# A decoder layer with pooling mixer and RWKV-7: the recurrent state added by an identity product, eight down products alone at the change of passes, the final norm of the first half issued later, two output tiles written ahead of a norm

## The chip, the cores and the metric

The kernel runs on one core of one Trainium2 chip. The metric is the device time of one execution in microseconds (us). The engines of the core work side by side, each through its own list of instructions in order: PE (TensorE, matrix products), DVE (VectorE), ACT (ScalarE), POOL (GpSimd) and SP (SyncE, which here only starts DMA transfers). PEld is the part of PE that loads weights; it works beside the products.

## What is computed

One layer for 1024 prompt tokens and 8 decode tokens, model width 1024, everything in fp32:

```
proj = rmsnorm(x) @ w_in                  # split into a pooling part and an RWKV part
pool = mean over trailing windows of 2/4/8/16 tokens, minus the token, times pool_w
rwkv: per head, token by token, with a 64x64 state S:
    sa = S @ a_t
    S  = S * w_t + sa b_t + v_t k_t       # w_t: decay
    y  = S @ r_t
x = x + concat(pool, rwkv) @ w_out
x = x + square(relu(rmsnorm(x) @ w_up)) @ w_down       # 1024 -> 4096 -> 1024
y = rmsnorm(x)
```

The outputs are y for prompt and decode tokens and the new states.

## The kernel before, in words

**Number format.** A product marked fp32r is cheap; an fp32 product costs more. The large products (projection `pj`, output `mx`, down `dn`) split each fp32 operand into a high and a low part and add three fp32r products (`gemm`, line 185). A weight tile arrives as `wr` (down, output, projection) or `a` (up), ACT writes its high part `wh` (line 94, the helper of all ACT work), DVE the low part `wl` (line 167 or 176). The small products of the recurrence are true fp32.

**Order.** The instructions are put in order by a list scheduler from the data they share; the order of the Python code is its priority, not the final order. Each engine then executes its list strictly in order.

**Stages.** (1) Projection and recurrence, up to about 466 us: the projection of one group of columns runs among the recurrence of the one before. The recurrence is cut into 8 units (4 pairs of heads, two halves of the tokens); `chain` runs one unit as 8 steps of 64 tokens, each step dependent on the one before, 64 steps in all. In a step, `SV` (128 x 128: two heads, block diagonal) is the state. `pq` = AR·SV goes to PSUM, ACT copies it to `Q`, `pa` = TT·Q goes to PSUM, ACT writes its diagonal blocks into `SV`, `pu` = BKT·SV goes to PSUM, and DVE writes the next state, `gam`·`pu` + `sg`. `sg` is `gam` times the old state, which ACT computes at the beginning of the step. `py` collects the output. All these PSUM tiles have the name `pcs` in the rows. Other PE work (projection, `bkt`, `vt` and others) is put between the products of a step by the scheduler.

(2) Up to about 568 us: the rest of the pooling mixer (`po`, with weights `pw`), the last unit, and the output projection of the first half of the tokens (`mx`).

(3) Output projection of the second half (`out_block`, 8 tiles m of two blocks each) with the second norm (`norm2`, sums `ss`, scale `rs2`) and the operands of the up product (`up_operands`) of the first half.

(4) The MLP in two passes over the halves: `up_pair(p)` is a seven-product scheme on blocks of `w_up` (products `b`, line 1014; combinations `a`, line 991; result `uh`, `ul`), and between its products it takes pieces of `down` (`dn`, added into `x` by DVE, line 1080) from a generator. Pairs 0 to 15 are the first half, 16 to 31 the second. At the change, `open_operands(1)` reloads the operands of the second half in 14 transfers on POOL's queue (line 932):

```
for t, d in zip(XO[half][i], XD[i]):
    GP.dma_start(t, d)
```

In group G == 7 four of the eight `down` tiles are drained ahead of `up_pair(16)`, and the other four are given to it. Behind that stands the final norm of two 256-column blocks of the first half (line 1086).

Of the kernel before, what the change touches and what calls it, by code (L numbers as in the profile page):

```python
# [7 lines left out]
F32 = mybir.dt.float32  # L8
F32R = mybir.dt.float32r
AF = mybir.ActivationFunctionType  # L10
ALU = mybir.AluOpType
# [4 lines left out]
P = 128  # L16
# [70 lines left out]
def _build(ctx, nc, tc, I, O, dbg):  # L87
    V, A, PE, SY, GP = nc.vector, nc.scalar, nc.tensor, nc.sync, nc.gpsimd
# [4 lines left out]
    def act(out, in_, func=AF.Copy, bias=0.0, scale=1.0, **k):  # L93
        A.activation(out, in_, func, bias=bias, scale=scale, **k)  # L94

    def open_pool(stack, name, bufs=1, **k):
        return stack.enter_context(tc.tile_pool(name=name, bufs=bufs, **k))

    R = (slice(0, 64), slice(64, 128))
# [13 lines left out]
    ident = cst[:, C_ID:C_ID + 128]  # L113
# [18 lines left out]
    def rstd(out, ps, ms, tmp):  # L132

        act(ms, ps, AF.Identity, bias=EPS6, scale=1.0 / D)
        act(tmp, ms, AF.Ln)
        act(out, tmp, AF.Exp, scale=-0.5)
        V.tensor_tensor(tmp, out, out, op=ALU.mult)
        V.scalar_tensor_tensor(tmp, tmp, -0.5, ms, ALU.mult, ALU.mult)
        V.scalar_tensor_tensor(out, tmp, 1.5, out, ALU.add, ALU.mult)
# [51 lines left out]
    rcp = open_pool(st_left, "rcp", reuse_waits="tile")  # L191
# [386 lines left out]
    def chain(U):  # L578
        hp = U.hp
        z1 = Zt[U.half][2]  # L580
        for i in range(2):
            nm = f"{hp}_{2 * U.half + i}"
            AR, RB, BKT, SV, TT = U.AR[i], U.RB[i], U.BKT[i], U.SV[i], U.TT
            if i == 0:
                for h in range(2):
                    if U.half == 0:
                        GP.memset(SV[R[h], 0, h, :], 0.0)
                    else:
                        act(SV[R[h], 0, h, :], Sf[hp][R[h], :])
            pyp = ps_y.tile([P, 512], F32, tag="y", name=f"py{nm}")  # L590
            py = pyp.rearrange("p (c h t) -> p c h t", h=2, t=64)
            for c in range(4):
                g = 4 * i + c
                gn = f"{U.nm}_{g}"
                sg = rcp.tile([P, 2, 64], F32, tag="sg", name=f"sg{gn}", bufs=2)
                act(sg, SV[:, c, :, :], scale=U.gam[:, g:g + 1])

                o = 256 * (hp % 2)
                pq, pa = (pcs[:, o + 128 * q:o + 128 * q + 128].rearrange("p (h t) -> p h t", t=64) for q in range(2))
                pu = pq  # L600
                PE.matmul(pq, AR[:, c, 0, :, :], SV[:, c, :, :], start=True, stop=True)  # L601
                PE.matmul(py[:, c, :, :], SV[:, c, :, :], AR[:, c, 1, :, :], start=True, stop=False)
                Q = rcp.tile([P, 2, 64], F32, tag="Q", name=f"Q{gn}", bufs=2)
                act(Q, pq)
                PE.matmul(pa, TT[:, g, :, :], Q, start=True, stop=True)  # L605
                for h in range(2):
                    act(SV[R[h], c, h, :], pa[R[h], h, :])
                PE.matmul(pu, BKT[:, c, :, :], SV[:, c, :, :], start=True, stop=True)  # L608
                PE.matmul(py[:, c, :, :], SV[:, c, :, :], RB[:, c, :, :], start=False, stop=True)
                for h in range(2):  # L610
                    if g == 7:
                        dst = Sf[hp][R[h], :]
                    elif c == 3:
                        dst = U.SV[1][R[h], 0, h, :]
                    else:
                        dst = SV[R[h], c + 1, h, :]
                    V.scalar_tensor_tensor(dst, pu[R[h], h, :], U.gam[R[h], g:g + 1], sg[R[h], h, :], ALU.mult, ALU.add)
            ys = rcp.tile([P, 256], F32, tag="ys", name=f"ys{nm}", bufs=2)
            for h in range(2):
                act(ys[R[h]].rearrange("p (c t) -> p c t", t=64), py[R[h], :, h, :])  # L620
            post(hp, nm, pyp, ys, 256, U.bv[:, 256 * i:256 * i + 256], z1[:, 256 * i:256 * i + 256], ys)
            QM.dma_start(mix_d[4 + hp][U.half][:, 256 * i:256 * i + 256], ys)
        if U.half:
            QM.dma_start(O["wkv_p"][hp], Sf[hp])
# [243 lines left out]
    def x1s(m, c, n):  # L868

        h = int(c >= 512)  # L870
        return x1[h][:, m, c - 512 * h:c - 512 * h + n]
# [39 lines left out]
    xtmp = lambda x, n: hq.tile([P, 260], F32, tag="xt", name=x, bufs=NXT)[:, :n]  # L911

    def norm2(c, n, tmp):

        ss = ps_m.tile([P, 512], F32, tag="m", name=f"ss2{c}")
        acc = tmp(f"acc2{c}")[:, :n]
        for m in range(KT):
            sq = tmp(f"sq2_{c}_{m}")[:, :n] if m else acc
            act(sq, x1s(m, c, n), AF.Square)
            if m:  # L920
                V.tensor_tensor(acc, acc, sq, op=ALU.add)
        PE.matmul(ss[:, :n], ON, acc, start=True, stop=True)
        rstd(rs2[:, c:c + n], ss[:, :n], tmp(f"ms2{c}")[:, :n], tmp(f"tt2{c}")[:, :n])
# [10 lines left out]
    def up_operands(half, k):  # L934

        c0, n = HALF[half]
        q = n // 2
        b = {}

        def normed(i, kk, o):  # L940
            b[i] = xtmp(f"b{i}_{k}_{half}", q)
            V.scalar_tensor_tensor(b[i], x1s(kk, o, q), col(V_G2, kk), rs2[:, o:o + q], ALU.mult, ALU.mult)

        def put(i, x):
            if half:
                h, l = (mp.tile([P, 260], F32R, tag=f"xs{y}", name=f"xs{i}{y}{k}", bufs=2) for y in "hl")
            else:
                h, l = (t[:, k, :q] for t in XO[half][i])
            act(h, x)
            V.tensor_tensor(l, x, f32(h), op=ALU.subtract)  # L950
            if half:
                for t, d in zip((h, l), XD[i]):
                    GP.dma_start(d[:, k, :], t)

        def less(i, x, y, out):
            V.tensor_tensor(b[out], b[x], b[y], op=ALU.subtract)
            put(i, b[out])

        normed("11", k, c0)
        put("11", b["11"])  # L960
        normed("21", k + 4, c0)
        put("21", b["21"])
        normed("12", k, c0 + q)
        less("t1", "12", "11", "11")
        normed("22", k + 4, c0 + q)
        put("22", b["22"])
        less("t2", "22", "11", "11")
        less("t3", "22", "12", "12")
        less("t4", "21", "11", "21")
# [80 lines left out]
    with tc.tile_pool(name="opb", bufs=1, reuse_waits="tile") as op:  # L1050
        ops = [mixed(op, k, 1, 3) for k in range(KT - 1)]
        load_x1(1)
        for c in (0, 256):
            norm2(c, 256, lambda x: xtmp(x, 260))
        open_operands(0)
        for m in range(KT):
            w = weights(I["w_out"][m, :, :(KT - 1) * P])
            for o in (0, 260):
                out_block(m, w, ops, 1, o, 260)
            if m % 2:  # L1060
                up_operands(0, m // 2)
        last = [mixed(op, KT - 1, 1, 3)]
        w7 = [w for m in (0, 4) for w in weights(I["w_out"][m:m + 4, :, (KT - 1) * P:].rearrange("m p c -> p m c"))]
        for m in range(KT):
            for o in (0, 260):
                out_block(m, w7[m:m + 1], last, 1, o, 260)
# [42 lines left out]
    for G in range(15):  # L1109
        first, rest = downs(G, range(4)), downs(G, range(4, 8))  # L1110
        if G == 1:
            for c, n in BLK[1:]:
                norm2(c, n, tmp)
        if 2 <= G < 6:
            up_operands(1, G - 2)
        if G == 7:
            open_operands(1)
            for _ in first:
                pass
        up_pair(2 * G + 2, rest if G == 7 else first)  # L1120
        up_pair(2 * G + 3, () if G == 7 else rest)
        if G == 7:
            for c in (0, 256):
                ss = ps_m.tile([P, 512], F32, tag="m", name=f"ss30{c}")[:, :256]
                acc = tmp(f"acc30{c}", "acc")[:, :256]
                for m in range(KT):
                    sq = tmp(f"sq3_{c}_{m}")[:, :256] if m else acc
                    act(sq, x1s(m, c, 256), AF.Square)
                    if m:
                        V.tensor_tensor(acc, acc, sq, op=ALU.add)  # L1130
                PE.matmul(ss, ON, acc, start=True, stop=True)
                for x in final_scale((c, 256), ss):
                    final(*x)
# [6 lines left out]
    for b in (1, 2):  # L1140
        c, n = BLK[b]
# [88 lines left out]
```

## Time and profile before

| | |
|---|---|
| median of 3 runs | 1336.54 us (1336.04 to 1337.41) |
| the profiled execution: its time, its span | 1335.81 us, 1334.0 us |
| mean granted clock of TensorE | 0.991 of full |
| PE busy | 1267.3 us, 95% of the span |
| PEld busy | 1146.4 us, 86% |
| DVE busy | 1050.9 us, 79% |
| ACT busy | 822.5 us, 62% |
| POOL busy | 125.4 us, 9% |
| DMA | 143.19 MB, mean 107 GB/s |

The span runs from the first to the last instruction of the profiled execution; some 1.8 us of its time lie around it. A row of the timeline gives start, duration, engine, line, operation, output<-inputs, shape, and in brackets how long the engine stood idle before it and what ended the wait. Shares of busy time are means over stages that are limited by different things.

### The profile page before, as it was taken

How to read it: one execution, taken by the hardware profiler on the slowest of the kernel's cores; microseconds unless marked ns; L12 is line 12 of the kernel's file. 1: busy time of each engine (PE TensorE's matmuls, PEld its weight loads, DVE VectorE, ACT ScalarE, POOL GpSimd, SP SyncE). 2: the span in 40 equal slices, each digit the busy share in tenths (PEclk: the TensorE clock that was granted, in tenths of full speed). 3: DMA queues.
4: the chain of work that ended last, by engine and by line, in shares of the span. 5: the costliest groups of instructions: out<-in, count | busy, mean ns of one | idle time of the engine just before them, and what ended most of it. 6: DMA issues, size and time to landing. Idle time of an engine off the chain costs nothing.

```text
span 1334.0 us, 27179 instructions
## 1 busy us (share of the span) xinstructions
PE 1267.3 (95%) x10230; PEld 1146.4 (86%) x10230; DVE 1050.9 (79%) x2331; ACT 822.5 (62%) x2015; POOL 125.4 (9%) x248
## 2 busy tenths in 40 slices
PE   5999999899999989989999999999899999999996
PEld 5987788798777867789989888998799999999996
DVE  8897687778877756589989997786698787878775
ACT  7668677776777657364757564555465645455552
POOL 4101001210011021110002320001000000000000
PEclk9999999999999989999999999999899999999999
DMA  6323123222222253442335663335634323332321
GB/s 209 102 54 83 43 50 90 95 93 53 66 56 48 63 164 135 142 149 80 119 115 150 181 167 96 113 97 186 217 99 147 103 89 105 94 106 93 104 71 64
DMA packets 119492, 143.19 MB, mean 107 GB/s; under 512 B 55769, under 2 KB 71257, under 8 KB 119353
## 3 DMA queue, kind: packets, MB, share of 16 engines
q1 hardware_dynamic: 97184, 92.22, 23.7%
q0 software_dynamic: 20320, 47.39, 11.4%
q10 hardware_dynamic: 1856, 1.85, 0.4%
q8 instruction: 80, 1.31, 0.4%
q14 instruction: 52, 0.42, 0.1%
HBM read 120.68 MB, written 20.97 MB: 106 GB/s over the span
## 4 chain that ended last, share of the span: by engine, by line
PE 68%; ACT 12%; DVE 11%; DMA 5%; issue 4%; POOL 1%; SPq 0%; DVEq 0%; ACTq 0%; POOLq 0%
PE dn L185 23%; PE b L1014 21%; PE pj L185 8%; PE mx L185 4%; ACT SV L94 2%; DMA a<-in_w_up 2%; PE pcs L608 1%; PE sc L431 1%; ACT wh L94 1%; ACT TT L94 1%; PE pcs L605 1%; DVE tm L525 1%; PE pcs L601 1%; DVE wl L167 1%; PE bkt L445 1%
## 5 line engine op out<-in xcount | busy, mean ns | idle before, releaser
L185 PE MATMUL dn<-uh,wh 128*128 128x260 f32 (+1 forms) x736 | 237.7, 324 | 6.1 <-DVE x L1080 4.3
L185 PE MATMUL dn<-ul,wh 128*128 128x260 f32 (+1 forms) x736 | 237.4, 323 | 1.2 <-DVE ul L1025 1.2
L185 PE MATMUL dn<-uh,wl 128*128 128x260 f32 (+1 forms) x736 | 237.2, 323 | 1.0 <-DVE wl L167 1.0
L94 ACT ACTIVATE wh<-a 128x512 fp32r<-128x512 f32 x192 | 120.8, 629 | 161.3 <-PE dn L185 85.0
L94 ACT ACTIVATE wh<-wr 128x512 fp32r<-128x512 f32 x230 | 142.9, 622 | 98.6 <-PE dn L185 26.0
L185 PE MATMUL pj<-xh,wh 128*128 128x258 f32 (+3 forms) x576 | 172.3, 299 | 13.7 <-ACT wh L94 13.7
L167 DVE TENSOR_TENSOR wl<-wr,wh 128x512 fp32r<-128x512 f32 x230 | 155.7, 681 | 35.4 <-ACT wh L94 27.5
L185 PE MATMUL pj<-xl,wh 128*128 128x258 f32 (+3 forms) x576 | 170.3, 296 | 0.0
L185 PE MATMUL pj<-xh,wl 128*128 128x258 f32 (+3 forms) x576 | 170.0, 295 | 0.1
L185 PEld LDWEIGHTS dn<-uh,wh 128*128 128x128 f32 x736 | 138.9, 189 | 17.3 <-ACT uh L94 3.2
L185 PEld LDWEIGHTS dn<-uh,wl 128*128 128x128 f32 x736 | 138.8, 189 | 12.3 <-DVE wl L167 1.2
L185 PEld LDWEIGHTS dn<-ul,wh 128*128 128x128 f32 x736 | 138.9, 189 | 10.8 <-DVE ul L1025 1.8
L176 DVE TENSOR_TENSOR wl<-a,wh 128x512 fp32r<-128x512 f32 x192 | 131.3, 684 | 6.2 <-ACT wh L94 3.6
L1080 DVE TENSOR_TENSOR x<-dn,x 128x260 f32<-128x260 f32 (+1 forms) x192 | 97.6, 511 | 41.5 <-PE dn L185 39.9
L185 PEld LDWEIGHTS pj<-xh,wh 128*128 128x128 f32 x576 | 109.9, 191 | 17.6 <-ACT wh L94 13.7
L185 PEld LDWEIGHTS pj<-xl,wh 128*128 128x128 f32 x576 | 110.0, 191 | 2.3 <-issue 1.9
L185 PEld LDWEIGHTS pj<-xh,wl 128*128 128x128 f32 x576 | 109.8, 191 | 1.8 <-issue 1.0
L94 ACT ACTIVATE c<-c 128x256 f32<-128x256 f32 (+1 forms) x128 | 53.1, 415 | 45.7 <-DVE c L1029 45.2
L991 DVE TENSOR_TENSOR a<-a,a 128x512 f32<-128x512 f32 x96 | 66.2, 689 | 19.0 <-DMA a<-in_w_up 17.5
L1025 DVE TENSOR_TENSOR ul<-u,uh 128x256 fp32r<-128x256 f32 (+1 forms) x128 | 53.6, 423 | 18.8 <-ACT uh L94 18.4
L185 PE MATMUL mx<-mh,wh 128*128 128x260 f32 (+1 forms) x192 | 64.9, 341 | 3.3 <-ACT mh L94 1.9
L185 PE MATMUL mx<-ml,wh 128*128 128x260 f32 (+1 forms) x192 | 63.6, 332 | 0.9 <-DVE ml L881 0.9
(421 smaller groups left out, 3388.6 us busy)
## 6 DMA issues: line engine op xcount, KB each, us to landing
a<-in_w_up SPq DMA_DIRECT2D x128, 256.0 KB, 2.6
wr<-in_w_down SPq DMA_DIRECT2D x128, 256.0 KB, 2.6
wr<-in_w_in POOLq DMA_DIRECT2D x72, 256.0 KB, 3.1
wr<-in_w_out POOLq DMA_DIRECT2D x26, 256.0 KB, 3.2
xr<-in_xT SPq DMA_DIRECT2D x16, 256.0 KB, 3.6
mr<-mix SPq DMA_DIRECT2D x8, 260.0 KB, 4.3
x<-in_xT SPq DMA_DIRECT2D x4, 520.0 KB, 5.0
blk<-AA SPq DMA_DIRECT2D x16, 128.0 KB, 2.7
```

Of the source, the lines that this page charges most:

```text
L94: A.activation(out, in_, func, bias=bias, scale=scale, **k)
L167: V.tensor_tensor(l[:, :w], raw[:, :w], f32(h[:, :w]), op=ALU.subtract)
L176: V.tensor_tensor(l, raw, f32(h), op=ALU.subtract)
L185: PE.matmul(ps, lhs, rhs, start=i == 0, stop=i == n - 1)
L431: PE.matmul(psc[:, c, :], BK[:, c, 2 * h:2 * h + 2, :], AR[:, c, :, h, :], start=True, stop=True)
L445: PE.transpose(pt[:, c, :], BK[:, c, 2 * h:2 * h + 2, :].rearrange("p a t -> p (a t)"), ident)
L525: V.tensor_tensor(pr[:, q], l[:, q].unsqueeze(2).to_broadcast([64, m, m, m]), r[:, q].rearrange("p k j -> p j k").unsqueeze(1).to_broadcas ...
L601: PE.matmul(pq, AR[:, c, 0, :, :], SV[:, c, :, :], start=True, stop=True)
L991: V.tensor_tensor(a[out], a[x], a[y], op=op)
L1014: PE.matmul(ps, lhs[:, c], rhs, start=k == i == 0, stop=k == 3 and i == 2)
L1025: V.tensor_tensor(ul, u, f32(uh), op=ALU.subtract)
L1080: V.tensor_tensor(d, ps[:, :n], d, op=ALU.add)
```

## The change

Four edits. In `chain` the tile `sg` is gone; the old state is added by a product of the identity matrix with `SV`, as first product of the group in `pu`, and DVE only multiplies by `gam`. In the output projection of the second half, `norm2` of the first half is written behind tiles 0 and 1, and the four `up_operands` behind tiles 3, 5, 6 and 7. In group 7 all eight `down` tiles are drained ahead of `up_pair(16)`. The final norm of the first half stands at group 9.

```
-                sg = rcp.tile([P, 2, 64], F32, tag="sg", name=f"sg{gn}", bufs=2)
-                act(sg, SV[:, c, :, :], scale=U.gam[:, g:g + 1])
...
                 PE.matmul(pa, TT[:, g, :, :], Q, start=True, stop=True)
+                PE.matmul(pu, ident, SV[:, c, :, :], start=True, stop=False)
                 for h in range(2):
                     act(SV[R[h], c, h, :], pa[R[h], h, :])
-                PE.matmul(pu, BKT[:, c, :, :], SV[:, c, :, :], start=True, stop=True)
+                PE.matmul(pu, BKT[:, c, :, :], SV[:, c, :, :], start=False, stop=True)
...
-                    V.scalar_tensor_tensor(dst, pu[R[h], h, :], U.gam[R[h], g:g + 1], sg[R[h], h, :], ALU.mult, ALU.add)
+                    V.tensor_scalar(dst, pu[R[h], h, :], U.gam[R[h], g:g + 1], None, ALU.mult)
...
-        for c in (0, 256):
-            norm2(c, 256, lambda x: xtmp(x, 260))
         open_operands(0)
         for m in range(KT):
...
-            if m % 2:
-                up_operands(0, m // 2)
+            if m == 1:
+                for c in (0, 256):
+                    norm2(c, 256, lambda x: xtmp(x, 260))
+            if m > 2 and m != 4:
+                up_operands(0, (0, 1, 2, 3)[(3, 5, 6, 7).index(m)])
...
             for _ in first:
                 pass
-        up_pair(2 * G + 2, rest if G == 7 else first)
-        up_pair(2 * G + 3, () if G == 7 else rest)
-        if G == 7:
+            for _ in rest:
+                pass
+        up_pair(2 * G + 2, first)
+        up_pair(2 * G + 3, rest)
+        if G == 9:
```

The scheduler decides where this lands. On PE, the third step of one unit in the recurrence, before (L605 is `pa`, L608 `pu`; `pj` and `vt` are other work):

```order
L601 MATMUL pcs<-SV_0_1709,AR_137 128x128
L602 MATMUL py_0_3513<-AR_137,SV_0_1709 128x128
L449 MATMUL vt_1_2392<-cst,v_0_2058 128x128
L185 MATMUL pj_1_2628<-xh_205,wl 128x256
L185 MATMUL pj_1_2654<-xh_205,wh 128x256
L185 MATMUL pj_1_2654<-xl_206,wh 128x256
L605 MATMUL pcs<-Q_0_2_3544,TT_157 128x128
L185 MATMUL pj_1_2654<-xh_205,wl 128x256
L185 MATMUL pj_1_2654<-xh_205,wh 128x256
L185 MATMUL pj_1_2654<-xl_206,wh 128x256
L185 MATMUL pj_1_2654<-xh_205,wl 128x256
L608 MATMUL pcs<-SV_0_1709,BKT_0_1708 128x128
```

and the same step of the change, where the lines are L599, L603 and L607 and the identity product is L604 (`cst` holds the identity):

```order
L599 MATMUL pcs<-SV_0_1701,AR_137 128x128
L600 MATMUL py_0_3497<-AR_137,SV_0_1701 128x128
L185 MATMUL pj_1_2638<-xh_205,wh 128x256
L185 MATMUL pj_1_2638<-xl_206,wh 128x256
L603 MATMUL pcs<-Q_0_2_3524,TT_157 128x128
L604 MATMUL pcs<-SV_0_1701,cst 128x128
L185 MATMUL pj_1_2638<-xh_205,wl 128x256
L185 MATMUL pj_0_2695<-xh_171,wh 128x256
L185 MATMUL pj_0_2695<-xl_172,wh 128x256
L185 MATMUL pj_0_2695<-xh_171,wl 128x256
L607 MATMUL pcs<-SV_0_1701,BKT_0_1700 128x128
L608 MATMUL py_0_3497<-RB_141,SV_0_1701 128x128
```

The identity product stands directly behind `pa`, ahead of the other work.

On ACT, the end of the squares (`sq`) and the scale (`ms`, `tt`, `rs`) of the second norm among the operands `mh` of the output projection of the second half, before:

```order
L94 ACTIVATE sq_0_7_7147<-x_6510 128x256
L94 ACTIVATE ms_7151<-ss_7126,sm 128x256
L94 ACTIVATE mh_1_7081<-mr_1_7080 128x520
L94 ACTIVATE tt_7152<-ms_7151 128x256
L94 ACTIVATE mh_1_7087<-mr_1_7086 128x520
L94 ACTIVATE rs_7059<-tt_7152 128x256
L94 ACTIVATE mh_1_7093<-mr_1_7092 128x520
```

and of the change:

```order
L94 ACTIVATE sq_0_7_7213<-x_6446 128x256
L94 ACTIVATE ms_7217<-ss_7192,sm 128x256
L94 ACTIVATE mh_1_7017<-mr_1_7016 128x520
L94 ACTIVATE tt_7218<-ms_7217 128x256
L94 ACTIVATE mh_1_7023<-mr_1_7022 128x520
L94 ACTIVATE rs_6995<-tt_7218 128x256
L94 ACTIVATE mh_1_7029<-mr_1_7028 128x520
```

Only the numbers of the tiles differ.

On DVE at the change of passes, from the sum of the last `down` tile of group 6 (`dn_7`) to that of the first of group 7 (`dn_0`), before (`c` belongs to the last pair of the first half, `a_16` is a combination of `w_up` for the first pair of the second half):

```order
L1080 TENSOR_TENSOR x_6510<-dn_7_0_11968,x_6510 128x512
L167 TENSOR_TENSOR wl<-wr,wh 128x512
L1029 TENSOR_TENSOR c_15_11999<-u_15_11914,b_15_11982 128x256
L176 TENSOR_TENSOR wl<-a_16_12142,wh 128x512
L991 TENSOR_TENSOR a_16_12142<-a_16_12144,a_16_12142 128x512
L1025 TENSOR_TENSOR ul_11781<-u_15_12001,uh_11780 128x256
L1029 TENSOR_TENSOR c_15_12023<-u_15_11953,b_15_12006 128x256
L176 TENSOR_TENSOR wl<-a_16_12148,wh 128x512
L991 TENSOR_TENSOR a_16_12148<-a_16_12148,a_16_12142 128x512
L1025 TENSOR_TENSOR ul_11779<-u_15_12025,uh_11778 128x256
L1080 TENSOR_TENSOR x_6510<-dn_0_0_12064,x_6510 128x512
```

and of the change:

```order
L1080 TENSOR_TENSOR x_6446<-dn_7_0_11904,x_6446 128x512
L167 TENSOR_TENSOR wl<-wr,wh 128x512
L1028 TENSOR_TENSOR c_15_11935<-u_15_11850,b_15_11918 128x256
L167 TENSOR_TENSOR wl<-wr,wh 128x512
L1028 TENSOR_TENSOR c_15_11959<-u_15_11889,b_15_11942 128x256
L1024 TENSOR_TENSOR ul_11717<-u_15_11937,uh_11716 128x256
L167 TENSOR_TENSOR wl<-wr,wh 128x512
L1024 TENSOR_TENSOR ul_11715<-u_15_11961,uh_11714 128x256
L1080 TENSOR_TENSOR x_6446<-dn_0_0_12000,x_6446 128x512
```

The four rows on `a_16` are gone from between the `c` and `ul` rows of the last pair, and two more low parts of `down` weights stand there.

## Rows read from the trace of the kernel before

**Rows 1.** The page: the share of the span in which PE was busy, and the shares of the engines in the chain that ended last.
```profile
PE 1267.3 (95%) x10230; PEld 1146.4 (86%) x10230; DVE 1050.9 (79%) x2331; ACT 822.5 (62%) x2015; POOL 125.4 (9%) x248
PE 68%; ACT 12%; DVE 11%; DMA 5%; issue 4%; POOL 1%; SPq 0%; DVEq 0%; ACTq 0%; POOLq 0%
```

**Rows 2.** Busy time by stage. Columns: stretch, its length, then busy time (number of instructions) of PE, PEld, DVE, ACT, POOL, the granted clock of PE, the DMA share, GB/s.
```profile
66.00:466.00 400.00, 379.44 (x3805) 325.39 (x3804) 313.40 (x777) 292.80 (x823) 45.98 (x95) 1.00 0.25 66
466.00:568.00 102.00, 93.10 (x651) 71.87 (x650) 58.36 (x122) 56.73 (x176) 17.28 (x32) 0.95 0.48 150
568.00:627.00 59.00, 54.60 (x426) 52.01 (x427) 54.85 (x135) 30.59 (x70) 4.74 (x8) 1.00 0.39 123
921.00:961.00 40.00, 35.51 (x184) 29.66 (x183) 22.55 (x44) 16.78 (x35) 7.42 (x14) 0.91 0.82 272
```

**Rows 3.** The timeline of PE in one step of the recurrence (start, duration).
```profile
349.01 0.49 PE L608 MATMUL pcs<-SV,BKT 128*128 128x128 f32 x2
349.34 0.39 PE L609 MATMUL py<-RB,SV 128*128 128x128 f32 x2
349.56 0.60 PE L445 MATMUL bkt<-cst,BK 128*128 128x128 f32 x4
...
350.37 0.46 PE L601 MATMUL pcs<-SV,AR 128*128 128x128 f32 x2
350.67 0.39 PE L602 MATMUL py<-AR,SV 128*128 128x128 f32 x2
350.89 0.38 PE L445 MATMUL bkt<-cst,BK 128*128 128x128 f32 x2
351.20 0.49 PE L605 MATMUL pcs<-Q,TT 128*128 128x128 f32 x2
```

**Rows 4.** The timeline of ACT in the same step.
```profile
350.48 0.39 ACT L94 ACTIVATE sg<-SV,gam 128x128 f32<-128x128 f32 x1
350.87 0.28 ACT L94 ACTIVATE Q<-pcs 128x128 f32<-128x128 f32 x1
```

**Rows 5.** The timeline of PE and ACT in another step, in which `sg` had ended early.
```profile
203.77 0.39 PE L601 MATMUL pcs<-SV,AR 128*128 128x128 f32 x2
204.19 0.28 ACT L94 ACTIVATE Q<-pcs 128x128 f32<-128x128 f32 x1 [0.26 <-PE pcs L601]
204.52 0.49 PE L605 MATMUL pcs<-Q,TT 128*128 128x128 f32 x2
```

**Rows 6.** Groups of instructions over the span: count | busy us, mean ns of one | idle us of the engine before them, and what ended most of it.
```profile
L608 PEld LDWEIGHTS pcs<-SV,BKT 128*128 128x128 f32 x128 | 19.9, 190 | 19.3 <-ACT SV L94 18.3
L605 PEld LDWEIGHTS pcs<-Q,TT 128*128 128x128 f32 x128 | 19.7, 188 | 12.0 <-ACT Q L94 7.2 <-ACT TT L94 2.3 <-issue 0.2
L601 PEld LDWEIGHTS pcs<-SV,AR 128*128 128x128 f32 x128 | 20.3, 188 | 11.0 <-DVE SV L617 6.7 <-issue 1.0 <-DVE Sf L617 0.4
L94 ACT ACTIVATE sg<-SV,gam 128x128 f32<-128x128 f32 x64 | 25.0, 396 | 20.4 <-DVE SV L617 20.1
L617 DVE SCALAR_TENSOR_TENSOR SV<-pcs,gam,sg 64x64 f32<-64x64 f32 x112 | 31.7, 283 | 27.3 <-PE pcs L608 26.0
L525 DVE TENSOR_TENSOR tm<-Xs,tw 64x64 f32<-64x64 f32 x16 | 3.6, 256 | 0.2
```

**Rows 7.** Around the start of the output projection of the second half: the window 565 to 570 us (columns as in rows 2), rows of PE's timeline, and two issues on SP's queue.
```profile
565.00:570.00 5.00, 1.84 (x9) 1.14 (x9) 2.75 (x5) 3.19 (x8) 0.54 (x1) 1.00 0.68 200
566.90 0.67 PE L922 MATMUL ss<-acc,cst 128*128 128x256 f32 x2 [1.78 <-DVE acc L921]
568.72 0.51 PE L185 MATMUL mx<-mh,wh 128*128 128x260 f32 x2 [1.15 <-ACT mh L94]
564.91 0.38 SPq L866 DMA_DIRECT2D x<-in_xT  x1
569.43 0.32 SPq L879 DMA_DIRECT2D mr<-mix  x1
```

**Rows 8.** The handover from projection to output: a window and a row of PE's timeline.
```profile
475.00:480.00 5.00, 0.58 (x65) 0.48 (x55) 0.69 (x1) 3.25 (x9) 0.33 (x1) 0.83 0.98 365
479.96 2.10 PE L783 MATMUL po<-d,pw 128*128 128x256 f32 x4 [4.42 <-DMA pw<-in_pool_w]
```

**Rows 9.** The change of passes: the first of the 14 reloads on POOL, rows of DVE's and PE's timelines, and two pieces of the chain of waits (start, length, what).
```profile
921.61 0.53 POOL L932 DMA_DIRECT2D x11l<-xd11l  x1 [127.69 <-PE b L1014]
939.41 0.69 DVE L991 TENSOR_TENSOR a<-a,a 128x512 f32<-128x512 f32 x1 [5.03 <-DMA a<-in_w_up]
948.28 0.69 DVE L176 TENSOR_TENSOR wl<-a,wh 128x512 fp32r<-128x512 f32 x1
941.78 0.47 PE L185 MATMUL dn<-uh,wh 128*128 128x512 f32 x1 [0.67 <-DVE x L1080]
945.45 0.48 PE L185 MATMUL dn<-uh,wh 128*128 128x512 f32 x1 [2.04 <-DVE x L1080]
949.76 1.22 PE L185 MATMUL dn<-uh,wh 128*128 128x512 f32 x2 [1.78 <-ACT uh L94]
949.76 9.96 PE dn L185 x36
978.08 13.01 PE b L1014 x108
```

**Rows 10.** The final norm of the first half: eight instructions of DVE, and the wait of PE behind them.
```profile
996.72 3.25 DVE L1086 SCALAR_TENSOR_TENSOR x<-x,vec,rs 128x256 f32<-128x256 f32 x8
1000.70 0.39 PE L185 MATMUL dn<-uh,wh 128*128 128x260 f32 x1 [1.59 <-DVE x L1080]
```

## The prediction

> **What bounds the kernel now.** I read the page first, then the busy time by stage, then the timelines where the change works. PE is busy 95% of the span and makes up 68% of the chain that ended last, ACT and DVE some 12% each [rows 1]: work taken from ACT or DVE is worth time only where PE waits for it, and work added to PE costs time wherever PE does not wait. The stages say where that is [rows 2]. In the recurrence, 66 to 466 us, PE works 379.4 of 400 us at full clock, so 20.6 us are all that could be won there, though the chain of 64 steps runs through it. From 466 to 568 us it loses 8.9 us, in the output projection of the second half 4.4 us, at the change of passes 4.5 us of 40 at a granted clock of 0.91. These four places are the ones that the edits touch.
>
> **The identity product.** 64 products of 128x128 by 128x128 in fp32 are added to PE. The price is in the timeline of one step, from start to start of neighbouring fp32 products of that size: 350.67 to 350.89 and 349.34 to 349.56, 0.22 us, and 0.33 us where the first of two has just ended a wait (349.01 to 349.34) [rows 3]. The new one follows `pa` directly, so it is a running stream: 0.22 us, 64 x 0.22 = 14.1 us. The bounds are 64 x 0.33 = 21.1 us, and nothing, if it only filled a wait. Can it? PE does wait for ACT's write of `SV` ahead of the third product of a step, 18.3 us in all [rows 6]. But the identity product reads the whole of `SV`, the old state, and ACT overwrites blocks of the same tile. ACT therefore has to wait until the product has read it. The order shows the product immediately behind `pa` and the other work behind it, in about the former number. So ACT starts 0.22 us later, `SV` comes 0.22 us later, and the wait keeps its length behind the new work. I take the full 14.1 us. The identity stands in `cst` already, so nothing is loaded for it.
>
> **What ACT gives back.** `sg` takes 25.0 us of ACT, 64 x 0.396 [rows 6], and starts when DVE has written the state, as `pq` does; `Q` waits behind it. In the step at 350 us `sg` ends at 350.87 and `Q` starts then, 0.50 us after its product started (350.37) [rows 3, 4]. In the step at 204 us, with ACT free, `Q` starts 0.42 us after its product (203.77 to 204.19) [rows 5]. So 0.08 us are saved in a step, 64 x 0.08 = 5.1 us. Nothing (where other ACT work holds `Q` up, or PE has work to cover it) and 7.2 us (all that PE's weight loads wait for `Q` [rows 6]) are the bounds.
>
> **What DVE gives back.** The new `tensor_scalar` reads PSUM and a scalar per partition, and is not in the trace of before in that form. The old instruction takes 283 ns with one tile from PSUM and one from SBUF; an addition of two 64x64 tiles takes 256 ns [rows 6]. A second operand is no large part of either; I take 27 ns less, the distance of the two rows. Two such instructions end a step, 2 x 27 ns x 64 = 3.5 us; they matter where PE waits for DVE's state, 6.7 us, so not in every step, and I take 1.5 us. Bounds: nothing, and the 6.7 us. The Trainium skill, page "VectorE: DVE Perf Modes", section "Why PSUM operands drop a tier", says that an fp32 operand in PSUM keeps DVE at its slowest mode whatever else is read; by it the term is zero and the sum 1.5 us higher. No run here shows yet which of the two holds.
>
> **The norm and the out tiles.** The loss is real: in 565 to 570 us PE works 1.84 us of 5, first waiting for the sum of squares, then for `mh` [rows 7]. If the two tiles ran ahead of the norm, they would fill it. The order of the change, however, has on ACT the same sequence as before, the squares, `ms`, then the first `mh`, word for word but for tile numbers; the scheduler puts the norm in front again, since it is ready and the tiles are not. They need `x` and `mr`, whose transfers SP issues only at 564.91 and 569.43 us [rows 7]. So this edit is worth nothing, and its cover is not taken away either. The bounds are the loss in that window, 3.2 us, and with the whole loss of the following stage [rows 2] 3.2 + 4.4 = 7.6 us.
>
> **The handover.** Before the output projection PE stands still from about 475.5 to 480 us, at the end waiting 4.42 us for the pooling weights `pw`, while the DMA engines are full (0.98) [rows 8]. The scheduler shuffles work there (part of the last unit's small products, and two `mr` loads earlier on SP). What is issued to the full DMA engines does not become less; I take 0, with that wait as the bound on either side, 4.4 us.
>
> **The change of passes.** The 14 reloads begin at 921.61 us on POOL [rows 9] and fill the DMA engines (share 0.82 over 40 us [rows 2]). The combinations of `w_up` come late: DVE stands still 5.03 us until 939.41 us for one. DVE then has its queue to work off, and PE waits 0.67, 2.04 and 1.78 us for DVE's `x` and for the last `uh` [rows 9]: 4.5 us, the whole loss of the stage. The clock of 0.91 costs another 0.09 x 40 = 3.6 us, together 8.1 us. What do eight down products ahead change? The order on DVE has the same late `a` rows ahead of `x<-dn_7`; behind it, four rows on `a_16` of 0.69 us each [rows 9] give way to two `wl<-wr`, so the last `ul` comes 2 x 0.69 = 1.4 us sooner. I take 1.4 us; the bounds are all 8.1 us, and a loss of 1.4 us if the two `down` weights now needed sooner are late in the full DMA engines. Behind that nothing is to be won: the three down products that PE works off from 949.76 us cover the reloads already, and `b` then follows without a wait. The four downs that leave `up_pair(16)` are the same instructions in another place, and the pairs alone run as tightly as up products did before where they stood alone, 108 products in 13.01 us [rows 9].
>
> **The final norm.** Eight DVE instructions in one piece of 3.25 us hold up the sums of `dn`, and PE waits 1.59 us behind them [rows 10]. At group 9 the same eight stand among the same kind of work. 0, with 1.6 us either way.
>
> **The sum.** 14.1 - 5.1 - 1.5 - 1.4 = +6.1 us, from the profiled 1335.81 us to 1341.9. The median of the runs is 0.73 us above the profiled execution, so **1342.6 us** on that scale.
>
> **The rivals.**
> (a) Nothing is given back. PE has other work in most steps, and a `Q` that comes 0.08 us sooner finds PE at a product of 0.3 us. That wait for `Q` is 7.2 us of 400 speaks for it. +14.1: 1350.6 us.
> (b) DVE gains nothing from the lost operand, by the form of the instruction: 14.1 - 5.1 - 1.4 = +7.6: 1344.1 us. This is what the page on DVE would make of it.
> (c) The other side: the identity product lies in a wait after all. If ACT's write does not stand behind it, or the scheduler's filling shrinks by as much in the steps where PE idles (18.3 us in all ahead of `pu`), its effective price is zero and the time falls to 1336.54 - 8.0 = 1328.5 us. It decides from a price below 0.125 us a product (8.0 / 64), and makes the kernel measurably faster below 0.08. Against it stands that the product reads what ACT then writes.
> (d) The change of passes loses its whole stall because DVE has only weights of `down` to split: 14.1 - 5.1 - 1.5 - 8.1 = -0.6: 1335.9 us. Against it: DVE is late because of `a` rows that stand ahead in both.
> (e) The two tiles do run ahead of the norm on the chip: 6.1 - 3.2 to 6.1 - 7.6, 1339.4 to 1335.0 us. Against it stands the order.
>
> **How the numbers follow.** A difference under 0.2% (2.7 us) can't be told from none here, so the borders are 1333.9 and 1339.2 us. Chances: the forecast 0.33 (own range 1338 to 1346), (a) 0.18, (b) 0.12, (c) 0.15, (d) 0.12, (e) 0.10. Faster: 0.13 of (c), 0.03 of (d), 0.01 of (e), together 0.17. The same: 0.06 of the forecast, 0.02 of (c), 0.09 of (d), 0.06 of (e), together 0.23. Slower: the rest, 0.60. The range is 1333 to 1351 us: it leaves out (c) for the most part and the upper end of the price of the product, and holds the others.
>
> **What would show it.** In the new profile PE's busy time in the recurrence grows by 14 us and its stretch by about 7.5 us; PE's idle time ahead of `pu` on ACT's `SV` stays near 18 us; that ahead of `pa` falls by some 5 us of the 7.2 for `Q`; the DVE instruction reads near 256 ns. The window at 565 us looks as before, and the waits at 941 to 950 us are there, shorter by about 1.4 us. The prediction is wrong if the stretch of the recurrence does not grow, if PE's wait for `SV` shrinks by as much as the new products take, or if the change of passes moves by more than 3 us.

## The result: slower by 1.2%, more than twice the forecast loss

The changed kernel takes 1352.11 us in the median of 4 runs (1349.59 to 1355.3), the kernel before 1336.88 us (1336.04 to 1337.41). The ratio is 1.0118, 95% interval [1.0103, 1.0133], or some 15.8 us. The forecast was +6.1 us. The profiled execution of the change is its fastest, 1349.59 us (span 1347.8, clock 0.992); the other runs of it had granted clocks of 0.983 to 0.987.

First the page of the change, the same parts as [rows 1]:

```profile
PE 1281.3 (95%) x10358; PEld 1160.8 (86%) x10358; DVE 1050.2 (78%) x2331; ACT 804.8 (60%) x1951; POOL 125.2 (9%) x248
PE 69%; ACT 9%; DVE 7%; issue 7%; DMA 4%; POOL 2%; POOLq 0%; DVEq 0%; SPq 0%; ACTq 0%
```

PE worked 14.0 us longer, with 128 instructions more (64 fp32 products of two each), and the span grew by 13.8 us. ACT worked 17.7 us less and DVE 0.7 us less.

By stage, cut at the last product of the projection and at the same later places. Before (columns as in [rows 2]):

```profile
56.00:471.70 415.70, 395.10 (x3926) 340.11 (x3925) 326.48 (x806) 299.99 (x838) 48.16 (x100) 1.00 0.26 66
471.70:568.00 96.30, 87.40 (x605) 66.17 (x603) 55.14 (x116) 54.66 (x172) 15.65 (x29) 0.95 0.46 151
```

and of the change (the third row answers to the third of [rows 2]):

```profile
56.40:483.10 426.70, 407.38 (x4038) 352.46 (x4037) 326.96 (x806) 285.00 (x781) 47.57 (x100) 1.00 0.25 64
483.10:580.90 97.80, 88.69 (x621) 67.40 (x620) 54.87 (x116) 52.87 (x165) 16.11 (x30) 0.97 0.49 152
580.90:638.20 57.30, 55.21 (x426) 53.13 (x427) 54.64 (x135) 30.26 (x70) 4.72 (x8) 0.97 0.39 126
```

The recurrence grew by 11.0 us: PE's busy time by 12.28 us for 56 added products (112 instructions), 0.219 us each, while PE's idle time there went from 20.6 to 19.3 us. The next stretch grew by 1.5 us, the output projection of the second half became 1.7 us shorter. Between their last row and the end lie 707.0 us before and 709.6 us after; with 0.4 us at the start these make the 13.8 us.

What PE waited for in a step, and what DVE's instruction takes now (L607, L603, L599 are `pu`, `pa`, `pq`; columns as in [rows 6]):

```profile
L607 PEld LDWEIGHTS pcs<-SV,BKT 128*128 128x128 f32 x128 | 19.6, 190 | 19.0 <-ACT SV L94 17.8 <-issue 0.5 <-ACT tailS L94 0.2
L603 PEld LDWEIGHTS pcs<-Q,TT 128*128 128x128 f32 x128 | 20.0, 190 | 12.5 <-ACT Q L94 7.7 <-ACT TT L94 1.5 <-issue 0.5
L599 PEld LDWEIGHTS pcs<-SV,AR 128*128 128x128 f32 x128 | 19.9, 189 | 7.7 <-DVE SV L616 4.0 <-issue 1.0 <-ACT SV L94 0.4
L616 DVE TENSOR_SCALAR SV<-pcs,gam 64x64 f32<-64x64 f32 x112 | 31.7, 283 | 33.2 <-PE pcs L607 31.7
```

The wait for `SV` is as long as before, 17.8 instead of 18.3 us. The wait for `Q` did not fall, 7.7 instead of 7.2 us. DVE takes 283 ns, exactly as before. The wait for DVE's state fell from 6.7 to 4.0 us all the same.

At the change of passes, PE and ACT of the change (answering to PE's rows in [rows 9]):

```profile
953.52 0.47 PE L185 MATMUL dn<-uh,wh 128*128 128x512 f32 x1 [0.52 <-DVE x L1080]
957.18 0.47 PE L185 MATMUL dn<-uh,wh 128*128 128x512 f32 x1 [2.04 <-DVE x L1080]
963.22 0.79 PE L185 MATMUL dn<-uh,wh 128*128 128x512 f32 x1 [4.87 <-ACT uh L94]
```

```profile
961.34 0.63 ACT L94 ACTIVATE wh<-wr 128x512 fp32r<-128x512 f32 x1 [2.03 <-DMA wr<-in_w_down]
961.88 0.40 ACT L94 ACTIVATE c<-c 128x256 f32<-128x256 f32 x1
962.31 0.42 ACT L94 ACTIVATE u<-c 128x256 f32<-128x256 f32 x1
962.75 0.42 ACT L94 ACTIVATE uh<-u 128x256 fp32r<-128x256 f32 x1
```

The wait for the last `uh` was 1.78 us and is 4.87 us. The last `uh` stands on ACT behind the high part of a `down` weight whose transfer landed late.

### The profile page after: what moved, and what is told of

Same layout as the page of the kernel before. It is cut to its first block, busy times and chain, and to the rows that moved or that the text cites. A ratio compares the mean times of both kernels' runs of the same rounds, so it can differ in the third digit from the quotient of the medians.

```text
span 1347.8 us, 27412 instructions
## 1 busy us (share of the span) xinstructions
PE 1281.3 (95%) x10358; PEld 1160.8 (86%) x10358; DVE 1050.2 (78%) x2331; ACT 804.8 (60%) x1951; POOL 125.2 (9%) x248
## 3 DMA queue, kind: packets, MB, share of 16 engines
q0 software_dynamic: 20320, 47.39, 11.4%
## 4 chain that ended last, share of the span: by engine, by line
PE 69%; ACT 9%; DVE 7%; issue 7%; DMA 4%; POOL 2%; POOLq 0%; DVEq 0%; SPq 0%; ACTq 0%
PE dn L185 21%; PE b L1013 18%; PE pj L185 9%; PE mx L185 6%; PE pcs L607 2%; PE sc L431 2%; ACT SV L94 2%; PE pcs L603 1%; ACT TT L94 1%; PE pcs L599 1%; DVE tm L525 1%; DMA a<-in_w_up 1%; ACT wh L94 1%; DVE x L1086 1%; PE bkt L445 1%
## 5 line engine op out<-in xcount | busy, mean ns | idle before, releaser
L185 PE MATMUL pj<-xh,wh 128*128 128x258 f32 (+3 forms) x576 | 173.0, 300 | 14.6 <-ACT wh L94 14.1
L185 PEld LDWEIGHTS pj<-xh,wh 128*128 128x128 f32 x576 | 110.0, 191 | 18.6 <-ACT wh L94 14.1
L990 DVE TENSOR_TENSOR a<-a,a 128x512 f32<-128x512 f32 x96 | 66.1, 689 | 19.4 <-DMA a<-in_w_up 17.9
```

The source lines that it names most:

```text
L185: PE.matmul(ps, lhs, rhs, start=i == 0, stop=i == n - 1)
L990: V.tensor_tensor(a[out], a[x], a[y], op=op)
```

## The experiments

All times are against the kernel before on the same chip; us are worked out from the ratio.

**Which edit.** The first edit alone, and the other three without it:

```
e1: sg and its add removed, identity product added      e2: norm order, eight downs, final norm
```

> Only the first edit: the identity product, without `sg` and with the shorter DVE instruction; the other three edits are left out. Theory A (the product costs its whole PE time, 64 x 0.22 = 14.1 us, and ACT and DVE give nothing back): +12 to +15 us against before. Theory B (ACT and DVE give back the 6.6 us that were predicted, and the other edits lose as much): +6 to +8.5 us.

Measured: 1.0123 [1.0106, 1.0141], +16.4 us, above the upper end of theory A.

> The other three edits without the first. Theory A (the identity product is nearly the whole loss): -1.5 to +2.5 us against before, with about +2.4 us at the change of passes, -1.6 us in the output projection of the second half and -0.5 us from the final norm, as between the two traces. Theory B (half of the loss is in these edits): +6 to +9 us.

Measured: 1.0017 [1.0006, 1.0028], +2.3 us. The identity product is nearly the whole loss; theory B falls. Each of the three others alone:

> Only the second edit, the norm and the up operands written later. If the order on the chip stays in front and only the later up operands help: -1 to -2 us, all of it before the first down product. If it does nothing, as predicted: within 0.5 us.

Measured: 0.9998 [0.9985, 1.0012]. Nothing that can be told. The 1.7 us won in the change's output projection don't appear as a gain of this edit.

> Only the third edit, eight down products alone. Theory: `uh` waits on ACT behind the high parts of `down` weights whose transfers land late among the 14 reloads; PE's wait for `uh` grows from 1.8 to about 4.9 us and the kernel loses 2 to 3 us. As predicted it would gain 1.4 us.

Measured: 1.003 [1.0017, 1.0042], +4.0 us. In its trace PE waits 2.86 us for `uh`, one us more than before, where 3 were expected; the profiled execution was 1336.92 us, the fastest of 12, so the trace shows the loss smaller than the runs do. The traces of e1 and e8, with four downs as before, have 2.70 us, so this wait alone does not show the loss:

```profile
943.71 0.47 PE L185 MATMUL dn<-uh,wh 128*128 128x512 f32 x1 [2.04 <-DVE x L1080]
947.74 0.79 PE L185 MATMUL dn<-uh,wh 128*128 128x512 f32 x1 [2.86 <-ACT uh L94]
```

> Only the fourth edit, the final norm at group 9. If the stall behind the norm only moves: within 1 us of before, the waits of about 2.6 us at 1000 and 1021 us gone and about as much in the pairs 22 and 23.

Measured: 1.0001 [0.9989, 1.0014]. The stall moves. In the trace of the change it is at pairs 22 and 23:

```profile
1100.68 0.39 PE L185 MATMUL dn<-uh,wh 128*128 128x260 f32 x1 [0.80 <-DVE x L1080]
1119.81 0.39 PE L1013 MATMUL b<-xt2h,wh 128*128 128x260 f32 x1 [0.60 <-ACT wh L94]
1120.98 0.39 PE L185 MATMUL dn<-uh,wl 128*128 128x260 f32 x1 [0.67 <-DVE wl L167]
```

**The price of the product, apart from what is given back.**

```
e3: -  act(sg, SV[:, c, :, :], scale=...)        # and tensor_scalar in place of the add of sg
e4: +  PE.matmul(pu, ident, SV[:, c, :, :], start=True, stop=True)      # behind pa
e5: +  PE.matmul(pa, ident, SV[:, c, :, :], start=True, stop=True)      # behind py, end of the step
```

> `sg` is gone and DVE only multiplies, but no identity product is added: the old state is left out of the sum, so the output is not the reference's. It measures what ACT and DVE give back, alone. Theory A: -1.5 to +0.5 us against before, the wait of PE for `Q` stays near 7 us. Theory B: -5 to -8 us, that wait falls to about 2 us.

Measured: 0.999 [0.9978, 1.0001], -1.3 us, not to be told from none. PE's wait for `Q` is 6.3 us: theory A. Its recurrence, and that wait (L602 is `pa` here):

```profile
56.50:470.50 414.00, 394.60 (x3927) 340.15 (x3926) 328.14 (x806) 282.61 (x781) 47.97 (x100) 1.00 0.25 66
L602 PEld LDWEIGHTS pcs<-Q,TT 128*128 128x128 f32 x128 | 19.9, 188 | 11.7 <-ACT Q L94 6.3 <-ACT TT L94 2.3 <-issue 0.2
```

> `sg` and the DVE instruction stay as before; the identity product is added at the place that it has in the change, into `pu`, and the next product overwrites it. It measures the price of the product alone. Theory A: +12.5 to +15 us, with 0.22 us more from `pa` to `pu` in a step. Rival C (it lies in a wait): under +5 us.

Measured: 1.0148 [1.0134, 1.0161], +19.8 us: more than both theories said.

> As the one before, but the added product stands behind the last product of the step, reads the new `SV` and writes the place of `pa` that nobody reads any more: the same PE work, outside of the chain of a step. If PE's time alone sets the price (PE is nearly always busy): +12.5 to +15 us, as inside the chain. If the price comes from the longer step (ACT's write waits 0.22 us more): +3 to +8 us, since the product then fills PE's waits.

Measured: 1.0089 [1.0075, 1.0104], +11.9 us, a little under the first alternative. But the product did not land outside of the chain. DVE waits for it (L610) before it writes the next state (L618):

```profile
L618 DVE SCALAR_TENSOR_TENSOR SV<-pcs,gam,sg 64x64 f32<-64x64 f32 x112 | 31.7, 283 | 23.2 <-PE pcs L610 19.4 <-PE vt L449 2.1
```

In all 64 steps that write starts at least 0.31 us behind the second instruction of the added product; it starts 0.83 us (median) behind the second instruction of `pu`, where it was 0.31 us before. So e5 also lengthens the step, at its end, and a product outside of the chain was not tested. By the runs the product is 8 us dearer behind `pa` than at the end of the step. The recurrence does not show that difference. Windows up to the last product of the projection, and on to the second half's output projection, of e4 and then of e5:

```profile
56.00:488.20 432.20, 408.99 (x4039) 355.31 (x4038) 326.49 (x805) 301.29 (x838) 47.98 (x100) 0.99 0.24 63
488.20:589.00 100.80, 88.33 (x621) 66.64 (x619) 55.06 (x116) 54.55 (x174) 15.93 (x30) 0.95 0.48 147
```

```profile
56.00:488.20 432.20, 410.02 (x4037) 355.99 (x4036) 327.34 (x806) 299.79 (x837) 47.80 (x99) 0.99 0.25 65
488.20:583.40 95.20, 89.35 (x621) 69.37 (x619) 54.68 (x116) 54.41 (x173) 15.69 (x29) 0.93 0.45 151
```

Both recurrences are 16.5 us longer than before, 432.2 against 415.7 us. PE's busy time grew by 13.9 and 14.9 us and its idle time did not fall. So the product's time on PE is paid in full at both places, and rival (c) is out; whether a product outside of the chain would fill PE's waits stays open. They part at the handover: 100.8 against 95.2 us (before 96.3). Why is not settled: each kernel has its own order there, and PE's idle time in that stretch is 12.5 us in e4 and 5.9 us in e5; the runs of e4 also had lower granted clocks, 0.984 to 0.988, than those of e5, 0.987 to 0.992.

**What `sg` was worth.**

```
e15: identity product and tensor_scalar as in the change; act(sg, ...) stays, used by nobody
```

> The first edit, but `sg` is still computed on ACT and used by nobody. If `sg` was hidden behind PE's product all along: the same as the first edit alone (+16.4 us), within 2 us. If taking `sg` away gave back time that the prediction rightly counted: 4 us or more slower than the first edit alone, +20 us or more against before.

Measured: 1.0169 [1.0136, 1.0201], +22.6 us, some 6 us slower than without `sg`. But the two intervals overlap (that of e1 reaches to 1.0141), and one of the six runs, 1369.41 us at a clock of 0.978, lies far above the others; by the medians, each against that of the kernel before beside it, the difference is 3.8 us. So it is not settled which of the two cases holds. The recurrence of e15, then that of e1:

```profile
56.50:485.70 429.20, 406.58 (x4040) 354.06 (x4039) 326.39 (x805) 301.27 (x838) 47.91 (x100) 1.00 0.24 64
56.50:484.60 428.10, 408.76 (x4036) 353.60 (x4035) 326.58 (x806) 284.71 (x780) 47.64 (x99) 1.00 0.25 64
```

PE idles 22.6 us in that of e15 (429.20 - 406.58); the same subtraction gives 23.2 us in e4, 20.6 us before, 19.3 us in e1 and in the change, and 19.4 us in e3 (414.00 - 394.60). So beside the added product there is 3 to 4 us less idle time without `sg`, and 1.2 us less where there is no added product. The stretch itself shows less of it: that of e15 is 1.1 us longer than that of e1 and 2.5 us longer than that of the change (426.70 us). And `Q` is not where it lies: PE's wait for `Q` is 6.2 us in e15 and 7.4 us in e1; what is longer in e15 are the waits ahead of the other two products. In the change all of this together leaves 1.3 us less idle time, and that is all that stands against the price.

**The change of passes.** Without reloads, with eight and four downs alone (the second pass uses the first one's operands):

```
-            open_operands(1)
+            XO[1].update(XO[0])          # and the four last columns set to zero
```

> Eight down products alone, and the 14 reloads are left out: the second pass works with the operands of the first, so the output is not the reference's. If the full DMA engines make the loss at the change of passes: PE's waits for `x` and `uh` there fall under 1 us in all and the kernel is 6 to 10 us faster than the one with eight down products and reloads (-3 to -7 us against before). If the order on DVE and ACT alone makes it: within 2 us of the one with reloads (+2 to +5 us against before).

> The same without reloads, but with four down products alone as before. If only the DMA makes eight dearer than four: the same time as with eight and no reloads, within 1.5 us. If the order does: 2 to 5 us faster than that.

Measured: both 0.9945, [0.9931, 0.9959] and [0.993, 0.9959], -7.4 us each. The loss comes with the reloads (eight downs are 11.4 us faster without them, more than the 6 to 10 expected), and without them four or eight downs are the same; in both traces PE has no wait over 0.3 us there. Then the reloads on SP's queue instead of POOL's, with eight (e10) and with four downs (e11):

```
-                    GP.dma_start(t, d)
+                    SY.dma_start(f32(t), f32(d))
```

e10 has a second difference, which e11 does not have: in the Python text the reloads stand behind the eight downs instead of ahead of them.

```
         if G == 7:
-            open_operands(1)
             for _ in first:
                 pass
...
+            for _ in rest:
+                pass
+            open_operands(1)
```

> Eight down products alone, and the reloads are issued on SP's queue among the weight loads instead of POOL's, so that the weights of the down products that are needed first are issued first. If late `down` weights hold up ACT and with it `uh`: PE's wait for `uh` falls under 2 us, 2 to 4 us faster than eight with the reloads on POOL (about +0 to +2 us against before). If SP is itself held up by the reloads' waits for free tiles: slower than that, +5 us or more.

Measured: 0.9941 [0.9928, 0.9954], -7.9 us: outside of both cases, better than expected, as good as no reloads. PE never stops there, and its granted clock is 1.00, though the DMA engines are about as full as before (0.81; the fourth row of [rows 2] has 0.82, with a clock of 0.91). The change at its change of passes, then this one:

```profile
932.90:972.90 40.00, 32.58 (x168) 27.21 (x167) 20.03 (x40) 15.95 (x33) 7.41 (x14) 0.91 0.84 279
920.00:960.00 40.00, 40.00 (x220) 34.16 (x220) 27.62 (x52) 20.78 (x43) 0.00 (x0) 1.00 0.81 286
```

One difference is the order of the loads. SP of the change, then SP of this one:

```profile
938.91 0.33 SPq L159 DMA_DIRECT2D wr<-in_w_down  x1
944.74 1.53 SPq L984 DMA_DIRECT2D a<-in_w_up  x2
952.80 6.13 SPq L159 DMA_DIRECT2D wr<-in_w_down  x5
```

```profile
934.10 0.33 SPq L159 DMA_DIRECT2D wr<-in_w_down  x1
936.93 1.82 SPq L159 DMA_DIRECT2D wr<-in_w_down  x2
941.13 0.33 SPq L159 DMA_DIRECT2D wr<-in_w_down  x1
944.67 2.44 SPq L985 DMA_DIRECT2D a<-in_w_up  x3
```

In the change two `a` loads come first, and no `down` weight is issued for 13.9 us; then five are, beside the last of the reloads. In e10 `down` weights stand between the reloads, and three `a` loads behind them. The order of the change is not new, though: the kernel before has it too, with 14.1 us without a `down` weight (927.01 to 941.06 us). The other difference is on DVE. In the change it stands still for an `a` load, as it did before (5.03 us, [rows 9]):

```profile
951.15 0.69 DVE L990 TENSOR_TENSOR a<-a,a 128x512 f32<-128x512 f32 x1 [5.24 <-DMA a<-in_w_up]
```

In e10 no wait of DVE there is longer than 1.6 us. The queue, the place of the reloads in the text, the order of the loads and DVE's order were not separated.

> The kernel before with four down products alone, and the reloads issued on SP's queue. If the queue is the cure: about as fast as eight with the reloads on SP, -6 to -8.5 us. If eight products are needed as cover once the order of the loads is right: -2 to -5 us.

Measured: 0.9964 [0.995, 0.9978], -4.8 us, the second case. But e10 and e11 also differ in the place of the reloads, and their intervals just overlap (e10 reaches up to 0.9954, e11 down to 0.995), so it is not shown that eight downs as cover gain the 3 us between them; without reloads they gain nothing over four (e12, e13). In e11 too no `down` weight is issued for 11.9 us (934.93 to 946.85 us), and yet PE waits only 1.1 us in all there, instead of 4.5. So late `down` weights alone do not make the stall. What e10, e11, e12 and e13 have in common is that DVE's wait of some 5 us for `a` is gone; that this is the cause was not tested.

**The final norm in pieces, and both together.** e9 hangs one square, sum or scale of the norm behind each down product; e14 joins it with e10.

> The kernel before with the final norm of the first half cut into pieces, one behind each down product from group 8 on, so that its eight DVE instructions no longer stand in one block. If the block is what holds PE up behind the norm: the waits at 1000 and 1021 us (2.6 us) go and don't come back, -2 to -4.5 us against before. If DVE lacks time as such: within 1 us.

Measured: 0.9968 [0.9956, 0.998], -4.3 us. The waits of [rows 10] are gone and don't come back. The 80 us from the end of the first pair of the second half, before and in e9:

```profile
981.00:1061.00 80.00, 77.25 (x632) 76.20 (x632) 70.25 (x154) 48.16 (x107) 0.00 (x0) 1.00 0.38 122
980.40:1060.40 80.00, 80.00 (x668) 79.95 (x667) 69.34 (x146) 50.26 (x111) 0.00 (x0) 1.00 0.37 115
```

> Eight down products alone, reloads on SP, and the final norm of the first half in pieces between the down products; no identity product. If the two gains are in different places, as the traces have them: -7.6 - 4.3 = about -11 to -12 us against before. If one uses up the other's: -8 to -9 us.

Measured: 0.9928 [0.9914, 0.9942], -9.6 us, 1326.31 us in the median: between the two cases, and faster than both kernels. By the traces the two parts do add up: from the last product of pair 15 to that of pair 17 it gains 7.2 us, from there to pair 19 another 4.9 us.

## Why the prediction was wrong, point by point

**The identity product: right.** 0.22 us was forecast for each, 0.219 us of busy time is measured in the recurrence; it does not fall into PE's wait for `SV`, which kept its length (17.8 instead of 18.3 us).

**What ACT gives back: the step that failed first.** 5.1 us were forecast. The reading of rows behind it mixed two things. In [rows 3, 5] the products have different lengths, 0.46 and 0.39 us. The change, without any `sg`, shows both distances again; PE and ACT in two of its steps:

```profile
113.09 0.49 PE L599 MATMUL pcs<-SV,AR 128*128 128x128 f32 x2
113.61 0.28 ACT L94 ACTIVATE Q<-pcs 128x128 f32<-128x128 f32 x1 [1.09 <-PE pcs L599]
```

```profile
127.50 0.38 PE L599 MATMUL pcs<-SV,AR 128*128 128x128 f32 x2
127.92 0.28 ACT L94 ACTIVATE Q<-pcs 128x128 f32<-128x128 f32 x1 [2.63 <-PE pcs L599]
```

`Q` starts 0.52 us after a long product has started, 0.42 us after a short one. So in the step that was read the 0.08 us were PE's own, and `sg` was hidden. In others it did hold `Q` up, as in this step of the kernel before:

```profile
400.90 0.38 PE L601 MATMUL pcs<-SV,AR 128*128 128x128 f32 x2
402.32 0.49 PE L605 MATMUL pcs<-Q,TT 128*128 128x128 f32 x2 [0.22 <-ACT Q L94]
```

```profile
401.58 0.39 ACT L94 ACTIVATE sg<-SV,gam 128x128 f32<-128x128 f32 x1
401.99 0.28 ACT L94 ACTIVATE Q<-pcs 128x128 f32<-128x128 f32 x1
```

In the trace of the kernel before 19 of the 64 `Q` start right behind `sg` and later than the 0.31 us behind the product's second instruction that is the least there, 8.5 us later in all. But without `sg` PE's wait for `Q` became little shorter (7.2 us before, 6.3 us in e3) or none (7.7 us in the change). And the saving of one step was multiplied by all 64, though PE's weight load waits for `Q` in 26 of them only. The change's idle time fell by 1.3 us in the recurrence, where ACT and DVE together were to give 6.6: rival (a) nearly.

**What DVE gives back: nothing by the instruction, where 1.5 us were forecast.** It takes 283 ns before and after. That agrees with what the Trainium skill, page "VectorE: DVE Perf Modes", section "Why PSUM operands drop a tier", says of an fp32 operand in PSUM; the rows decide for rival (b) on this term. That PE's wait for DVE's state fell from 6.7 to 4.0 us in the change is not the instruction's doing: in e3, with the same instruction and no added product, it is 7.2 us.

**The norm and the out tiles: right** that the norm stays in front, with the two waits of [rows 7] as they were, and that the edit alone is worth nothing (e6). PE of the change:

```profile
579.76 0.67 PE L921 MATMUL ss<-acc,cst 128*128 128x256 f32 x2 [1.78 <-DVE acc L920]
581.58 0.80 PE L185 MATMUL mx<-mh,wh 128*128 128x260 f32 x2 [1.15 <-ACT mh L94]
```

The change's own output projection was 1.7 us shorter; as the edit alone shows no gain, this is not put down to it.

**The handover: right within its bounds**, +1.5 us, of which 1.3 us are products of the last unit.

**The change of passes: wrong in sign.** -1.4 us was forecast; the end of pair 15 is 11.9 us late in the change and that of pair 16 is 14.3 us, so it loses 2.4 us, and the edit alone 4.0 us by the runs. The step looked at DVE's order only. The four rows did go from DVE, but in the change the wait moved to ACT, where `uh` stands behind the weights of the additional downs, and ACT waits 2.03 us for one of these. The text named that risk, late `down` weights, at 1.4 us. That wait of ACT is 1.20 us in the trace of e2; that of e7 has none and loses 1.3 us there, so where the 4.0 us of e7's runs lie no trace shows.

**The final norm: right**, the stall moved and cost about the same.

**The sum of the profiled execution:** from +6.1 us, the failed give-back adds 5.3, the change of passes 3.8; the product and the handover together take 0.3 us off (14.1 forecast, 13.6 of busy time and 0.2 of idle time measured), the output projection 1.7, the final norm 0.5, and the start and the first pass add 1.1: +13.8, the difference of the spans. The rest to the measured 15.8 us goes with the lower clocks of the change's other runs (0.983 to 0.987, the profiled one 0.992); that these are its cause is not shown. The forecast's range ended at 1351, because it held the full price, but not the full price and a loss at the change of passes at once.

## What to carry to other kernels

On an engine that is 95% busy, work added to its chain cost its full time here, and time given back by other engines counted only where a wait got shorter; compare two rows for such a gain only if the instruction ahead of them has the same length in both. Where transfers are in line behind one another, look at the queue that issues them and at who stands in line behind a late one: here the reloads on SP's queue were worth 4.8 us with four downs ahead, and 7.9 us with eight and the reloads behind them in the text. A block of work on a helper engine that held up a busy one was cured here by cutting it into pieces, not by moving it.

## What the runs showed of the hardware

An fp32 product of 128x128 by 128x128 added to a stream of others took 0.219 us of PE (12.28 us for 56, change against before). DVE took 283 ns for 64x64 fp32 from PSUM both with a second tile from SBUF (before) and without (the change). With the DMA engines at 0.81 to 0.84 of their time PE was at 40.00 of 40 us in e10 and at 32.58 in the change, with the reloads on another queue, in another place and order.
